# Third-group attention keys made by seven products in an earlier stage, with the scores woven into half projections

## The chip, the cores and the metric

The kernel runs on one core of a Trainium2 chip. The metric is the device time of one execution in microseconds; three runs of the kernel before gave 2182.49, 2182.76 and 2183.83 us, median 2182.76. A core has TensorE (PE, matrix products into PSUM; PEld are its weight loads), VectorE (DVE), ScalarE (ACT), GpSimd (POOL) and SyncE (SP, which here only issues DMAs). Each engine works through its own instructions in the order in which the program issued them, and waits on semaphores for the others.

## The reference

One decoder block on a sequence of 1024 tokens and width 1024, in float32: a token mixer and a squared-ReLU MLP, each behind an RMSNorm that is scaled and shifted by a conditioning vector. The mixer multiplies the normed input h by one wide matrix and cuts the result into retention queries, keys, values and gates (4 heads), attention queries, keys and values of three groups of 4 heads of 128 channels, and two gates. Cut to what matters here:

```
proj = h @ w_in
for gi, (win, dil) in enumerate(((128, 1), (512, 4), (2048, 16))):
    aq, ak, av = parts[4 + 3 * gi], parts[5 + 3 * gi], parts[6 + 3 * gi]
    # strided sub-sequences, banded blocks
    s = einsum(q, k) * dh ** -0.5 + bias
    mx = max(s); e = exp(s - mx); den = sum(e)
    o = einsum(e / den, v);  lse = mx + log(den)
wts = softmax over the three groups of lse
att = sum over groups of wts * o
att_out = att @ w_att_out
```

The kernel's "group 1" is the second one (dilation 4), "group 2" the third one (dilation 16), "group 0" the first.

## The kernel before, in words

A float32 product is made of three passes: both operands are split into a high part (a rounded copy, made by ScalarE) and a remainder (the difference, made by VectorE), and `mm3` (L203 to L211) issues low x high, high x low and high x high into one PSUM accumulation. A matmul takes 128 rows of weights by 512 tokens. A plain projection of one block of 128 channels, `proj_gen`, takes 8 slices of the width x 3 passes x 2 halves of the tokens = 48 matmuls.

The stages follow each other: values of attention; the **queries and keys stage** (`queries_keys`, L1212); retention values; 32 retention chunks; the **attention stage**; the gates and outputs; the MLP. They are one list of steps (`Steps`, L55). A step has loads of 512 KB tiles, each with a preparation (`split_w` for a weight, L194; `q_prep` for queries, L1475), and a body. All loads share three buffers (`wraw`) and go through SP's queue in order; a load is issued when the tile three places before it has been prepared (`issue`, L78). `following` (L114) issues the preparations of the next step, and of the step behind it the weights that come ahead of any other load, *before* the body of a step. So the splits of a step stand ahead of the body of the step before it in ScalarE's and VectorE's order.

**Queries and keys stage.** The stage computes two blocks of 128 channels at a time ("a pair") from a 2 x 2 blocking of weights and tokens by seven products of 12 matmuls, 84 in place of 96 (`Blocks`, L226; `ORDER`, L217 ff.). Per pair ScalarE and VectorE split 7 weight tiles of 512 columns (L254, L264), VectorE makes 4 sums of weights (L249) and combines the products (L286 to L293), and `a_out` (L1165) writes the four result blocks, for attention groups 1 and 2 in a strided order, and sends them to DRAM: retention queries and keys (`r`, behind which `rotate` applies the rotary embedding on VectorE, one instruction per product), attention queries (`a`, tiles `aqd`) and gates (`g`, sigmoid on ScalarE). `PAIRS` (L1136) gives the order of 18 pairs, "rargrargrargrargaa".

**Attention stage.** Heads are taken two by two ("attention pair" 0 and 1). For each of them there are six steps `att_step` (L1753), one for each group and head of `combos` (L1751): group 1, group 2, group 0, heads a = 0 and 1. A step projects the keys of its head with 48 matmuls, and weaves into them the scores of the head before (`weave`, from the third slice on: `lag=2`). `k_split` (L1484) then splits the keys out of PSUM. `scores_gen` (L1492) makes the scores bank by bank in four PSUM buffers and VectorE adds the bias (L1519, L1523); `scores_end` (L1526) reduces the maxima (L1529 to L1537), negates them (L1539) and lets ScalarE take eight exponentials (L1542). Queries come back from DRAM as loads. High and low parts of queries and keys live in a ring of 8 tiles (`ring`, L1405). After a group's second head `stats_out` (L1600) sends maxima and sums through DRAM on SP's queue. Behind the six steps come gate projections (`cover_step`, L1791: four in pair 0, three in pair 1). The first holds the last scores, then `weights` and `pscale` (L1645, L1647); the third holds the first group's weighted values (`weave_pv`, `pv_tr`, `pv_mm`: L1662 to L1688).

`with_sums` (L576) places one of 32 DMAs on POOL's queue after the second and the sixth slice of each projection; they add blocks of the retention output in DRAM (`result_sum`, L566).

Of the kernel before, what the change touches and what calls it, by code (L numbers as in the profile page):

```python
# [17 lines left out]
P = 128  # L18
# [122 lines left out]
def block_kernel(ctx, tc, io, stop=None, dbg=None):  # L141
# [24 lines left out]
    def ps_mm(name):  # L166
        return PS["p"].tile([P, 2, 512], F32, tag="mm", bufs=2, name=name)
# [314 lines left out]
    def at(gen, n, call):  # L482

        for i, _ in enumerate(gen):
            if i == n:
                call()
            yield
# [5 lines left out]
    def weave(main, n, fill, m, lag=0, rest=True):  # L493


        done = 0
        for i, _ in enumerate(main):
            while i >= lag and done * (n - lag) < (i + 1 - lag) * m:
                next(fill, None)
                done += 1  # L500
        if rest:
            drain(fill)
# [72 lines left out]

    def with_sums(gen):  # L576

        return at(at(gen, 1, result_sum), 5, result_sum)

    hd = {}  # L580
    NG = H * NC
# [187 lines left out]

    va_d = [dram.tile([S, 512], F32, name=f"vad{g}") for g in range(3)]  # L770
    aq_d = {(p, g, a): dram.tile([P, S], F32, name=f"aqd{p}{g}{a}") for p in range(2) for g in range(3) for a in range(2)}
    h12_d = [dram.tile([P, 2, 512], F32, name=f"h12d{m}") for m in range(4)]
    xn, wa = [], []

# [358 lines left out]
    r_pairs = [("r", t, h) for h in range(H) for t in "qk"]  # L1133
    a_pairs = [("a", g, p) for p in range(2) for g in range(3)]
    g_pairs = [("g", i) for i in range(len(GATES) // 2)]
    PAIRS = [{"r": r_pairs, "a": a_pairs, "g": g_pairs}[i].pop(0) for i in "rargrargrargrargaa"]  # L1136
    NA = len(PAIRS)
    OA = {}

    def a_load(q, part):  # L1140
        pair = PAIRS[q]
        src = io[{"g": "w_gate2", "a": "w_aq"}.get(pair[0]) or f"w_r{pair[1]}"]
        i = 2 * pair[1] + pair[2] if pair[0] == "a" else pair[-1]
        if q == 0 or q % 2 == 0 and part == 2:
            r = x4(f"wa{q}{part}")
        else:
            r = wraw.tile([P, 1024], F32, tag="raw", name=f"wa{q}{part}")
        nc.sync.dma_start(r, src[2 * i + part - 1])
        BA.raw[q, part] = r
# [15 lines left out]
    def a_out(q, n, x, y=None):  # L1165

        pair = PAIRS[q]
        if q not in OA:
            OA[q] = [x4(f"qa{q}{i}") for i in range(2)]
        i, t = int(n[0]) - 1, int(n[1]) - 1  # L1170
        o, view = OA[q][i][:, 512 * t:512 * t + 512], lambda z: z
        if pair[0] == "a" and pair[1] == 1:
            o = OA[q][i].rearrange("p (r n i) -> p r n i", r=4, n=2)[:, :, t, :]
            view = lambda z: z.rearrange("p (i r) -> p r i", r=4)
        elif pair[0] == "a" and pair[1] == 2:
            o = OA[q][i].rearrange("p (r i) -> p r i", r=8)[:, :, 64 * t:64 * t + 64]
            view = lambda z: z.rearrange("p (i r) -> p r i", r=8)
        f = AF.Sigmoid if pair[0] == "g" else AF.Copy
        if y is None:
            nc.scalar.activation(o, view(x), f)  # L1180
        else:
            (nc.vector.tensor_add if n == "12" else nc.vector.tensor_sub)(o, view(x), view(y))
            if pair[0] == "g":
                nc.scalar.activation(o, o, f)
        if n in ("12", "21"):
            if pair[0] == "g":
                dst = gate_d[GATES[2 * pair[1] + i]]
            elif pair[0] == "a":
                dst = aq_d[pair[2], pair[1], i]
            else:  # L1190
                return
            nc.sync.dma_start(dst, OA[q][i])
# [282 lines left out]
    def q_prep(pair, g, a):  # L1475
# [5 lines left out]
            A["q", g, a] = (hi, lo)  # L1481
        return prep

    def k_split(pair, g, a, ps):  # L1484

        hi, lo = ring(f"kh{pair}{g}{a}"), ring(f"kl{pair}{g}{a}")
        src, h_, l_ = by_blocks(ps, g), shaped(hi, g), shaped(lo, g)
        nc.scalar.copy(h_, src)
        nc.vector.tensor_sub(l_, src, fv(h_))
        A["k", g, a] = (hi, lo)  # L1490
# [70 lines left out]
    def v_fetch(pair, g):  # L1561

        for j in range(2):
            lo = A["l", g, j] = v_tile(pair, g, j, "vl")
            nc.sync.dma_start(fv(lo).rearrange("p (a b) -> p a b", a=4), v_rows(pair, g, j))
# [182 lines left out]
                done += 1  # L1748
        drain(main)

    combos = [(g, a) for g in (1, 2, 0) for a in range(2)]  # L1751

    def att_step(pair, i):  # L1753

        g, a = combos[i]

        def body(*args):
            ps = ps_mm(f"ak{pair}{i}")
            gen = with_sums(proj_gen(ps, args[-1]))
            if i == len(combos) - 2:  # L1760
                v_fetch(pair, 0)
            if i > 0:
                last = combos[i - 1]
                weave(gen, NK, scores_gen(pair, *last), len(SB[last[0]]), lag=2)
            elif pair == 0:
                args[0](1, True)
                for _ in range(4):
                    next(gen)
                on_T(H - 1, NC - 1)
                drain(gen)  # L1770
                u_final(H - 1)
                for h in range(H):
                    sums_left.extend(sums_of(h))
                open_att()
                args[0](3)
            else:

                gen = at(at(gen, 3, args[0]), NK - 1, lambda: k_split(pair, g, a, ps))
                weave_pv(gen, NK - 1, 0, 2)
            if i == 0:  # L1780
                A["st"] = A["p"].tile([P, 3, 8, 4], F32, tag="st", name=f"st{pair}")
                bias_load(pair)
            if i > 0 or pair == 0:
                k_split(pair, g, a, ps)
            if i > 0:
                scores_end(pair, *last)
                if last[1] == 1:
                    stats_out(pair, last[0])
        return body

    def cover_step(pair, n):  # L1791


        i = COVER[pair][n]

        def body(*args):
            ps = ps_mm(f"gate0{i}")
            gen = with_sums(proj_gen(ps, args[-1]))
            if n == 0:
                v_fetch(pair, 1)  # L1800
                weave(gen, 6, scores_gen(pair, *combos[-1]), len(SB[0]), lag=2, rest=False)
                drain(gen)
                v_split(pair, 0, False)
                scores_end(pair, *combos[-1])
                weights(pair)
                for a in range(2):
                    pscale(0, a)
            elif n == 1:
                drain(gen)
            elif n == 2:  # L1810
                v_fetch(pair, 2)

                gen = at(at(gen, 2, lambda: sigmoids(1)), 3, lambda: (args[0](3), v_split(pair, 1)))
                gen = at(gen, 6, sigmoids)
                weave_pv(gen, NK - 1, pair, 0)
                for a in range(2):
                    pscale(1, a)
            else:
                gen = at(at(gen, 3, lambda: [pscale(2, a) for a in range(2)]), 4, lambda: args[0](1))
                gen = at(at(at(gen, 6, lambda: v_split(pair, 2)), 6, args[0]), 6, sigmoids)  # L1820
                weave_pv(gen, NK - 1, pair, 1)
            if n > 1:
                t = A["r1"].tile([P, S], F32, tag="att", bufs=8, name=f"g0{i}s")
            else:
                t = ring(f"g0{i}s", F32)
            if n < 3:
                nc.vector.tensor_copy(t[:, :512], ps[:, 0])
                nc.scalar.copy(t[:, 512:], ps[:, 1])
                raw_gates.append((i, t))
            else:  # L1830
                nc.scalar.activation(t, flat(ps), AF.Sigmoid)
                nc.sync.dma_start(gate_d[i], t)
        return body
# [7 lines left out]
            nc.sync.dma_start(gate_d[i], t)  # L1841

    for pair in range(2):
        for i, (g, a) in enumerate(combos):
            steps.add(att_step(pair, i),
                      [wsplit(io["w_ak"][g * 4 + 2 * pair + a])] +
                      ([(aq_d[pair, *combos[i - 1]], q_prep(pair, *combos[i - 1]))] if i > 0 else []),
                      manual=("late" if pair else True) if i == 0 else False)
        for n in range(len(COVER[pair])):
            more = [(aq_d[pair, *combos[-1]], q_prep(pair, *combos[-1]))] if n == 0 else []  # L1850
            steps.add(cover_step(pair, n), more + [wsplit(io["w_gate"][len(COVER[0]) * pair + n])], manual={2: True, 3: "late"}.get(n, False))


# [897 lines left out]
def pack(x, c, w_ada, b_ada, norm1_g, w_in, rel_bias, ret_gn_g, ret_gn_b,  # L2751
# [16 lines left out]
        "w_rv": _vblocks(w[:, 2048:4096]),  # L2768
        "w_rg": _cols(w[:, 4096:6144]),
        "w_aq": _pairs(att[:, :, 0].reshape(1024, 1536)),  # L2770
        "w_ak": _cols(att[:, :, 1].reshape(1024, 1536)),
        "w_av": _vcols(att[:, 0, 2], 512),
        "w_av2": _vblocks(att[:, 1:, 2].reshape(1024, 1024)),
        "w_gate": _cols(gates(i for c in COVER for i in c)),
# [27 lines left out]
```

## Time and profile before

| | |
|---|---|
| median of three runs | 2182.76 us (2182.49 to 2183.83) |
| profiled execution | 2182.64 us, its span 2180.9 us |
| TensorE clock granted | 1.00 but for the start and the end |
| queries and keys stage | 180 to 523 us |
| attention stage, pair 0, six steps | 943.9 to 1024.6 us |
| attention stage, pair 1, first score step on | from 1111 us |
| HBM read, written | 319.93 MB, 156.13 MB |

A busy TensorE is a modelled figure: its matmuls overlap, so what counts is the distance from start to start. In an order of time each row has its start, duration, engine, line, operation and "output<-inputs", a count where rows are merged, and in brackets the idle time before it with what ended it. A row of DMA issues ends with the median microseconds from issue to landing.

### The profile page before, as it was taken

How to read it: one execution, taken by the hardware profiler on the slowest of the kernel's cores; microseconds unless marked ns; L12 is line 12 of the kernel's file. 1: busy time of each engine (PE TensorE's matmuls, PEld its weight loads, DVE VectorE, ACT ScalarE, POOL GpSimd, SP SyncE). 2: the span in 40 equal slices, each digit the busy share in tenths (PEclk: the TensorE clock that was granted, in tenths of full speed). 3: DMA queues.
4: the chain of work that ended last, by engine and by line, in shares of the span. 5: the costliest groups of instructions: out<-in, count | busy, mean ns of one | idle time of the engine just before them, and what ended most of it. 6: DMA issues, size and time to landing. Idle time of an engine off the chain costs nothing. (4 is left out here: it accounts for less than half of the span.)

```text
span 2180.9 us, 27323 instructions
## 1 busy us (share of the span) xinstructions
PE 2156.0 (99%) x10084; PEld 1791.6 (82%) x10084; DVE 1491.7 (68%) x2333; ACT 942.8 (43%) x1729; POOL 164.0 (8%) x195
## 2 busy tenths in 40 slices
PE   8999999999999999999999999999999999999998
PEld 6888888888878888888888888888778888888887
DVE  5985777774467877854655644776876665877855
ACT  5553323323434544544644625434454545533413
POOL 0001111100012212211100000001000000000003
PEclk9999999999999999999999999999999999999999
DMA  9859998844685555557763275654254435645322
GB/s 383 289 209 297 296 298 257 243 119 174 237 301 170 198 174 194 181 172 190 184 167 108 81 268 189 224 186 139 65 182 150 153 136 194 249 137 175 111 87 78
DMA packets 160881, 416.78 MB, mean 191 GB/s; under 512 B 27749, under 2 KB 55660, under 8 KB 157676
## 3 DMA queue, kind: packets, MB, share of 16 engines
q1 hardware_dynamic: 151416, 368.67, 47.9%
q0 software_dynamic: 9008, 46.14, 9.9%
q8 instruction: 79, 1.29, 0.2%
q14 instruction: 54, 0.44, 0.1%
q10 hardware_dynamic: 324, 0.23, 0.0%
HBM read 319.93 MB, written 156.13 MB: 218 GB/s over the span
## 5 line engine op out<-in xcount | busy, mean ns | idle before, releaser
L207 PE MATMUL qap<-hh,qaw 128*128 128x512 f32 x216 | 84.0, 389 | 0.0
L209 PE MATMUL qap<-hl,qaw 128*128 128x512 f32 x216 | 84.0, 389 | 0.0
L211 PE MATMUL qap<-hh,qaw 128*128 128x512 f32 x216 | 84.0, 389 | 0.0
L617 POOL TENSOR_TENSOR j<-qk,j 128x512 fp32r<-128x512 f32 x32 | 43.2, 1351 | 412.4 <-ACT j L616 393.8
L2122 POOL TENSOR_TENSOR accnf<-accnf,sqnf 128x256 f32<-128x256 f32 (+1 forms) x18 | 16.6, 922 | 609.9 <-ACT sqnf L2118 609.9
L2226 ACT ACTIVATE a<-a 128x512 f32<-128x512 f32 x48 | 30.3, 631 | 73.7 <-DVE a L2225 73.7
L1542 ACT ACTIVATE P<-P,ng 128x128 f32<-128x128 f32 (+1 forms) x96 | 42.0, 439 | 36.6 <-DVE ng L1539 36.6
L2434 ACT CAST w2h<-w2s 128x512 fp32r<-128x512 f32 x36 | 22.4, 622 | 78.7 <-DVE w2s L2472 78.7
L264 DVE TENSOR_TENSOR fw<-w1r,fw 128x512 fp32r<-128x512 f32 x48 | 32.9, 688 | 33.6 <-ACT fw L254 33.6
L1957 DVE TENSOR_TENSOR rwl<-rwl,rwh 128x1024 fp32r<-128x1024 f32 x25 | 30.2, 1220 | 29.1 <-ACT rwh L1987 29.1
L207 PE MATMUL fp<-h2h,fw 128*128 128x512 f32 x128 | 50.0, 391 | 0.0
L211 PE MATMUL fp<-h2h,fw 128*128 128x512 f32 x128 | 49.8, 389 | 0.0
L209 PE MATMUL fp<-h2l,fw 128*128 128x512 f32 x128 | 49.8, 389 | 0.0
L207 PE MATMUL roa<-rh,rwl 128*128 128x512 f32 x128 | 49.8, 389 | 0.0
L209 PE MATMUL roa<-rl,rwh 128*128 128x512 f32 x128 | 49.8, 389 | 0.0
L211 PE MATMUL roa<-rh,rwh 128*128 128x512 f32 x128 | 49.8, 389 | 0.0
L652 ACT COPY sm<-sT 128x128 f32<-128x128 f32 x32 | 8.5, 266 | 93.7 <-PE sT L640 93.7
L207 PEld LDWEIGHTS qap<-hh,qaw 128*128 128x128 f32 x216 | 40.5, 188 | 8.5
L209 PEld LDWEIGHTS qap<-hl,qaw 128*128 128x128 f32 x216 | 40.5, 188 | 8.4
L211 PEld LDWEIGHTS qap<-hh,qaw 128*128 128x128 f32 x216 | 40.5, 188 | 8.4
L2122 POOL TENSOR_TENSOR accn<-accn,sqn 128x512 f32<-128x512 f32 x12 | 15.5, 1293 | 386.1 <-ACT sqn L2118 386.1
L1947 ACT ACTIVATE rh<-rl 128x512 fp32r<-128x512 f32 x56 | 31.7, 623 | 23.4 <-PE roc L209 8.4
(3097 smaller groups left out, 7251.4 us busy)
## 6 DMA issues: line engine op xcount, KB each, us to landing
v<-vd SPq DMA_DIRECT2D x32, 512.0 KB, 4.5
raw<-in_w_ada_dram SPq DMA_DIRECT2D x32, 512.0 KB, 5.3
w1r<-in_w_ff_dram SPq DMA_DIRECT2D x32, 512.0 KB, 4.6
yt<-y POOLq DMA_DIRECT2D x24, 512.0 KB, 7.6
xsd<-as SPq DMA_DIRECT2D x24, 512.0 KB, 2.8
w2r<-in_w_ff2s_dram SPq DMA_DIRECT2D x24, 512.0 KB, 6.9
em<-in_w_ada_dram SPq DMA_DIRECT2D x16, 512.0 KB, 10.2
wrvs<-in_w_rv_dram POOLq DMA_DIRECT2D x16, 512.0 KB, 10.0
```

The source lines that it names most:

```text
L207: nc.tensor.matmul(o, wl, xh, start=first, stop=False, skip_group_check=skip)
L209: nc.tensor.matmul(o, wh, xl, start=False, stop=False, skip_group_check=skip)
L211: nc.tensor.matmul(o, wh, xh, start=False, stop=last, skip_group_check=skip)
L264: nc.vector.tensor_sub(t[:, 512:], src, fv(t[:, :512]))
L617: nc.gpsimd.tensor_sub(t[:, 1], src, fv(t[:, 0]))
L652: nc.scalar.copy(sm, ps[:, :C])
L1542: nc.scalar.activation(v, v, AF.Exp, bias=ng[:, blk:blk + 1], accum_out=st[:, g, blk, 2 + a:3 + a])
L1947: nc.scalar.activation(hi, fv(lo), AF.Copy, scale=sign)
L1957: nc.vector.tensor_sub(lo, fv(lo), fv(hi))
L2122: (nc.vector if f == 7 else nc.gpsimd).tensor_add(G["acc", key], G["acc", key], sq)
L2226: nc.scalar.activation(o, o, AF.Relu)
L2434: nc.scalar.copy(hi, src)
```

## The change

The keys of group 2 are taken out of the attention stage. Two `k` pairs in the queries and keys stage make them by seven products (weights in a new layout, `w_ak2`), in the strided order of that group, and store them in DRAM (`akd`). In the attention stage they come back as loads with a preparation of their own, `k_prep`.

So an attention pair has four key projections instead of six. Group 1's two stay whole steps. Group 0's two are cut into halves of four slices (`att_first`, `att_second`), and each half takes one head's scores, woven in from the second slice on (`lag=1`): group 1 head 1, group 2 head 0, group 2 head 1, group 0 head 0. The last scores stay in the first gate projection. The order of `PAIRS` changes too: 20 pairs, two gates moved to the end. `with_sums` places three sums per projection. The host only packs the weights.

```diff
-        return at(at(gen, 1, result_sum), 5, result_sum)
+        return at(at(at(gen, 1, result_sum), 3, result_sum), 5, result_sum)
...
-    PAIRS = [{"r": r_pairs, "a": a_pairs, "g": g_pairs}[i].pop(0) for i in "rargrargrargrargaa"]
+    k_pairs = [("k", 2, p) for p in range(2)]
+    PAIRS = [{"r": r_pairs, "a": a_pairs, "g": g_pairs, "k": k_pairs}[i].pop(0) for i in "rargrarkrargrarkgaga"]
...
-        elif pair[0] == "a" and pair[1] == 2:
+        elif pair[0] in "ak" and pair[1] == 2:
...
+            elif pair[0] == "k":
+                dst = ak_d[pair[2], i]
...
+    def k_prep(pair, a):
+
+        def prep(raw):
+            hi, lo = ring(f"kh{pair}2{a}"), ring(f"kl{pair}2{a}")
+            nc.scalar.copy(hi, raw)
+            nc.vector.tensor_sub(lo, raw, fv(hi))
+            A["k", 2, a] = (hi, lo)
+        return prep
...
+    HALF = NK // 2
+
+    def att_first(pair, a):
+
+        def body(*args):
+            A["kp"] = ps_mm(f"ak{pair}0{a}")
+            A["kg"] = with_sums(proj_gen(A["kp"], args[-1]))
+            done = (1, 1) if a == 0 else (2, 1)
+            if a == 1:
+                v_fetch(pair, 0)
+            weave(itertools.islice(A["kg"], HALF), HALF, scores_gen(pair, *done), len(SB[done[0]]), lag=1)
+            scores_done(pair, *done)
+        return body
+
+    def att_second(pair, a):
+
+        def body(*args):
+            done = (2, 0) if a == 0 else (0, 0)
+            weave(A["kg"], HALF, scores_gen(pair, *done), len(SB[done[0]]), lag=1)
+            k_split(pair, 0, a, A["kp"])
+            scores_done(pair, *done)
         return body
...
-        for i, (g, a) in enumerate(combos):
-            steps.add(att_step(pair, i),
-                      [wsplit(io["w_ak"][g * 4 + 2 * pair + a])] +
-                      ([(aq_d[pair, *combos[i - 1]], q_prep(pair, *combos[i - 1]))] if i > 0 else []),
-                      manual=("late" if pair else True) if i == 0 else False)
...
+        steps.add(att_step(pair, 0), [w_load(1, 0)], manual="late" if pair else True)
+        steps.add(att_step(pair, 1), [w_load(1, 1), q_load(1, 0)])
+        steps.add(att_first(pair, 0), [w_load(0, 0), q_load(1, 1)])
+        steps.add(att_second(pair, 0), [q_load(2, 0), k_load(0)])
+        steps.add(att_first(pair, 1), [w_load(0, 1), q_load(2, 1), k_load(1)])
+        steps.add(att_second(pair, 1), [q_load(0, 0)])
```

`scores_done` is `scores_end` followed by `stats_out` after a group's second head.

More of the change, by code (lines that the diff above doesn't have):

```diff
@@ L771, in block_kernel @@
     aq_d = {(p, g, a): dram.tile([P, S], F32, name=f"aqd{p}{g}{a}") for p in range(2) for g in range(3) for a in range(2)}
+    ak_d = {(p, a): dram.tile([P, S], F32, name=f"akd{p}{a}") for p in range(2) for a in range(2)}
     h12_d = [dram.tile([P, 2, 512], F32, name=f"h12d{m}") for m in range(4)]
@@ L1141, in a_load @@
         pair = PAIRS[q]
-        src = io[{"g": "w_gate2", "a": "w_aq"}.get(pair[0]) or f"w_r{pair[1]}"]
+        src = io[{"g": "w_gate2", "a": "w_aq", "k": "w_ak2"}.get(pair[0]) or f"w_r{pair[1]}"]
         i = 2 * pair[1] + pair[2] if pair[0] == "a" else pair[-1]
@@ L1171, in a_out @@
         o, view = OA[q][i][:, 512 * t:512 * t + 512], lambda z: z
-        if pair[0] == "a" and pair[1] == 1:
+        if pair[0] in "ak" and pair[1] == 1:
             o = OA[q][i].rearrange("p (r n i) -> p r n i", r=4, n=2)[:, :, t, :]
             view = lambda z: z.rearrange("p (i r) -> p r i", r=4)
-        elif pair[0] == "a" and pair[1] == 2:
+        elif pair[0] in "ak" and pair[1] == 2:
             o = OA[q][i].rearrange("p (r i) -> p r i", r=8)[:, :, 64 * t:64 * t + 64]
@@ L1749, in weave_pv, with scores_done, att_step @@
         drain(main)
-    combos = [(g, a) for g in (1, 2, 0) for a in range(2)]
-    def att_step(pair, i):
-        g, a = combos[i]
+    def scores_done(pair, g, a):
+        scores_end(pair, g, a)
+        if g > 0 and a == 1:
+            stats_out(pair, g)
+    def att_step(pair, a):
         def body(*args):
-            ps = ps_mm(f"ak{pair}{i}")
+            ps = ps_mm(f"ak{pair}1{a}")
             gen = with_sums(proj_gen(ps, args[-1]))
[L1760 to L1764, printed above, removed]
+            if a == 1:
+                weave(gen, NK, scores_gen(pair, 1, 0), len(SB[1]), lag=2)
             elif pair == 0:
@@ L1776, in body @@
             else:
-                gen = at(at(gen, 3, args[0]), NK - 1, lambda: k_split(pair, g, a, ps))
+                gen = at(at(gen, 3, args[0]), NK - 1, lambda: k_split(pair, 1, 0, ps))
                 weave_pv(gen, NK - 1, 0, 2)
-            if i == 0:
+            if a == 0:
                 A["st"] = A["p"].tile([P, 3, 8, 4], F32, tag="st", name=f"st{pair}")
                 bias_load(pair)
[L1783 to L1788, printed above, removed]
+            if a == 1 or pair == 0:
+                k_split(pair, 1, a, ps)
+            if a == 1:
+                scores_done(pair, 1, 0)
+        return body
[5 more added lines that the diff above has]
+            done = (1, 1) if a == 0 else (2, 1)
+            if a == 1:
+                v_fetch(pair, 0)
+            weave(itertools.islice(A["kg"], HALF), HALF, scores_gen(pair, *done), len(SB[done[0]]), lag=1)
+            scores_done(pair, *done)
+        return body
+    def att_second(pair, a):
[4 more added lines that the diff above has]
+            scores_done(pair, *done)
         return body
@@ L1800, in body @@
                 v_fetch(pair, 1)
-                weave(gen, 6, scores_gen(pair, *combos[-1]), len(SB[0]), lag=2, rest=False)
+                weave(gen, 6, scores_gen(pair, 0, 1), len(SB[0]), lag=2, rest=False)
                 drain(gen)
                 v_split(pair, 0, False)
-                scores_end(pair, *combos[-1])
+                scores_end(pair, 0, 1)
                 weights(pair)
@@ L1843, in block_kernel, with q_load, k_load, w_load @@
     for pair in range(2):
-        for i, (g, a) in enumerate(combos):
-            steps.add(att_step(pair, i),
-                      [wsplit(io["w_ak"][g * 4 + 2 * pair + a])] +
-                      ([(aq_d[pair, *combos[i - 1]], q_prep(pair, *combos[i - 1]))] if i > 0 else []),
-                      manual=("late" if pair else True) if i == 0 else False)
+        def q_load(g, a):
+            return aq_d[pair, g, a], q_prep(pair, g, a)
+        def k_load(a):
+            return ak_d[pair, a], k_prep(pair, a)
+        def w_load(g, a):
+            return wsplit(io["w_ak"][g * 4 + 2 * pair + a])
+        steps.add(att_step(pair, 0), [w_load(1, 0)], manual="late" if pair else True)
[4 more added lines that the diff above has]
+        steps.add(att_second(pair, 1), [q_load(0, 0)])
         for n in range(len(COVER[pair])):
-            more = [(aq_d[pair, *combos[-1]], q_prep(pair, *combos[-1]))] if n == 0 else []
+            more = [q_load(0, 1)] if n == 0 else []
             steps.add(cover_step(pair, n), more + [wsplit(io["w_gate"][len(COVER[0]) * pair + n])], manual={2: True, 3: "late"}.get(n, False))
@@ L2770, in pack @@
         "w_aq": _pairs(att[:, :, 0].reshape(1024, 1536)),
-        "w_ak": _cols(att[:, :, 1].reshape(1024, 1536)),
+        "w_ak": _cols(att[:, :2, 1].reshape(1024, 1024)),
+        "w_ak2": _pairs(att[:, 2, 1]),
         "w_av": _vcols(att[:, 0, 2], 512),
```

## The prediction

> **What bounds the kernel now.** I read the page's busy times first, then the windows of the two stages that the change touches, then ScalarE's, VectorE's and TensorE's order of time in the first attention pair.
>
> ```profile
> span 2180.9 us, 27323 instructions
> PE 2156.0 (99%) x10084; PEld 1791.6 (82%) x10084; DVE 1491.7 (68%) x2333; ACT 942.8 (43%) x1729; POOL 164.0 (8%) x195
> ```
> ```profile
> 180.00:523.00 343.00, 343.00 (x1515) 284.02 (x1514) 245.29 (x382) 100.01 (x174) 36.31 (x50) 1.00 0.79 238
> 969.60:1049.50 79.90, 79.90 (x410) 68.00 (x409) 45.70 (x77) 41.21 (x121) 9.41 (x14) 1.00 0.74 199
> 1122.40:1202.30 79.90, 79.90 (x411) 67.98 (x410) 43.99 (x74) 41.27 (x121) 0.82 (x1) 1.00 0.34 96
> 2175.00:2181.00 6.00, 0.00 (x0) 0.00 (x0) 1.97 (x4) 0.00 (x0) 0.00 (x0) 0.50 0.58 193
> ```
>
> The columns of a window are its length and the busy time (count) of PE, weight loads, DVE, ACT, POOL, then granted clock, DMA share and GB/s. TensorE is the bound everywhere: it is busy in all of the queries and keys stage (180 to 523) and in all of both attention stretches (the second and third row: from the third key product of a pair to its third gate product, 79.9 us each). 343.00 us for 1515 matmuls of 512 columns is **0.2264 us a matmul**. A change is worth what it takes off TensorE, as long as nobody makes TensorE wait.
>
> **The change, part by part.**
>
> *Matmuls.* Two pairs with seven products enter the queries and keys stage: 2 x 84 x 0.2264 = **+38.0 us**. Four full projections of 48 leave the attention stage: 192 x 0.2264 = **-43.5 us**. The difference is 24 matmuls, 5.4 us.
>
> *The queries and keys stage.* Does it take two more pairs at TensorE's pace?
>
> ```profile
> L1182 DVE TENSOR_TENSOR qa<-qat,qap x36: 677/686/1133, 192.6 to 523.0; 128x512 f32<-128x512 f32 x36
> ```
>
> A pair gives VectorE 4 sums, 7 remainders, 2 differences and 3 results, 16 x 0.69 = 11.0 us, and for the third group's strided order 3 x 0.45 more (1133 against 686 ns), 12.4 us of the pair's 84 x 0.2264 = 19.0. The rotation of the retention pair before it, 12 instructions spread over 14 products, puts up to 7 x 0.69 = 4.8 us beside it: 17.2 of 19.0, which the present pair of third-group queries behind a retention pair already bears without a TensorE gap. The gates that now end the list add sigmoids to ScalarE, which is busy for 100 of 343 us. SP issues two loads and two stores more per pair, as for any other pair. So +38.0 stands; if a product did come late, it would be by one VectorE instruction, 0.7 us, a few times.
>
> *The attention stage.* Here the 96 matmuls a pair that leave were also the cover for the scores. The next rows are ScalarE, VectorE and TensorE in the first pair.
>
> ```profile
> 978.01 1.04 ACT L1479 ACTIVATE qh<-raw 128x1024 fp32r<-128x1024 f32 x1
> 988.08 0.40 ACT L1542 ACTIVATE P<-P,ng 128x128 f32<-128x128 f32 x1 [3.22 <-DVE ng L1539]
> 991.61 1.04 ACT L1479 ACTIVATE qh<-raw 128x1024 fp32r<-128x1024 f32 x1
> 992.56 1.03 ACT L197 CAST raw_8378h<-raw 128x1024 fp32r<-128x1024 f32 x1
> 1001.19 0.40 ACT L1542 ACTIVATE P<-P,ng 128x128 f32<-128x128 f32 x1 [2.63 <-DVE ng L1539]
> 1004.29 1.05 ACT L1479 ACTIVATE qh<-raw 128x1024 fp32r<-128x1024 f32 x1
> 1029.68 0.41 ACT L1542 ACTIVATE P<-P,ng 128x128 f32<-128x128 f32 x1 [3.62 <-DVE ng L1539]
> 1033.53 1.04 ACT L197 CAST raw_8707h<-raw 128x1024 fp32r<-128x1024 f32 x1
> 1040.64 0.40 ACT L1542 ACTIVATE P<-P,ng 128x128 f32<-128x128 f32 x1 [4.17 <-DVE ng L1539]
> ```
> ```profile
> 981.36 1.88 DVE L1519 TENSOR_TENSOR P<-sc,bias 128x512 f32<-128x512 f32 x3
> 986.04 0.68 DVE L1534 TENSOR_REDUCE st<-P 128x4 f32<-128x512 f32 x1
> 992.69 1.23 DVE L1480 SCALAR_TENSOR_TENSOR ql<-raw,qh 128x1024 fp32r<-128x1024 f32 x1 [4.64 <-ACT qh L1479]
> 993.83 1.22 DVE L198 TENSOR_TENSOR raw_8378l<-raw,raw_8378h 128x1024 fp32r<-128x1024 f32 x1
> 994.97 1.28 DVE L1519 TENSOR_TENSOR P<-sc,bias 128x512 f32<-128x512 f32 x2
> 998.60 1.23 DVE L1489 TENSOR_TENSOR kl<-ak,kh 128x1024 fp32r<-128x1024 f32 x1 [2.35 <-ACT kh L1488]
> 999.74 1.21 DVE L1537 TENSOR_REDUCE st<-P 128x8 f32<-128x1024 f32 x1
> 1022.46 1.88 DVE L1519 TENSOR_TENSOR P<-sc,bias 128x512 f32<-128x512 f32 x3
> 1024.26 0.61 DVE L1523 TENSOR_TENSOR P<-sc,bias 128x256 f32<-128x256 f32 x2
> 1027.23 0.28 DVE L1529 TENSOR_REDUCE st<-P 128x1 f32<-128x128 f32 x1
> ```
> ```profile
> 997.30 0.62 PE L207 MATMUL ak<-hh,raw_8268l 128*128 128x512 f32 x2
> 1010.98 0.62 PE L207 MATMUL ak<-hh,raw_8378l 128*128 128x512 f32 x2
> 1054.51 0.39 PE L1687 MATMUL pv<-ptl000(0, 0, 0)_9051,vh 128*128 128x256 f32 x1 [0.34 <-DVE ptl000(0, 0, 0)_9051 L1667]
> ```
>
> The reader is to see a **loop through two engines**. The splits of the next step are issued ahead of a step's own scores, so the order is: ScalarE copies the high parts, VectorE takes the remainders, then VectorE adds the bias to the scores that TensorE made meanwhile, reduces them, ScalarE takes eight exponentials, and only behind these come the next copies (qh starts at 991.61 and 1004.29, where the exponentials end). The brackets are where an engine of the loop waits for the other one or for TensorE. Now each turn has a step of 1010.98 - 997.30 = 13.7 us of TensorE. In the changed kernel four of the steps have 24 matmuls and one head's scores: 13.7 - 24 x 0.2264 = 8.25 us. The copies that a turn holds are not fewer: the third group's keys come from DRAM and are split in place of its weights.
>
> From the rows, from start to start: first copy to first remainder 1.08; a remainder 1.14; a bias addition 0.60 (2.41 for the first group's five); the split of a product's keys on VectorE 1.14 (998.60 to 999.74); reduction to first exponential 2.04 for the second group (986.04 to 988.08), 1.45 for the third (999.74 to 1001.19), 2.45 for the first (1027.23 to 1029.68); exponentials 3.53, 3.10 and 3.85 (988.08 to 991.61, 1001.19 to 1004.29, 1029.68 to 1033.53). The turns of the changed kernel, from the end of the first head's exponentials:
>
> - A, three splits (third-group query and key, a weight), scores of the second group: 1.08 + 3 x 1.14 + 3 x 0.60 + 2.04 + 3.53 = 11.9
> - B, two splits, third group, keys of a product: 1.08 + 2.28 + 1.20 + 1.14 + 1.45 + 3.10 = 10.2
> - C, one split, third group: 1.08 + 1.14 + 1.20 + 1.45 + 3.10 = 8.0
> - D, three splits (a query, two gate weights), first group, keys of a product: 1.08 + 3.42 + 2.41 + 1.14 + 2.45 + 3.85 = 14.4
> - E, one split, first group, up to its first exponential: 1.08 + 1.14 + 2.41 + 2.45 = 7.1
>
> Together **51.5 us** with no idle time, of which TensorE wanted four times 8.25 for A to D. Before, the same way is 1040.64 - 978.01 = 62.6 us, idle time included. From the exponential at 1040.64 to the weighted values at 1054.51 the rest of the chain runs without a pause, and TensorE already waits 0.34 us at its end. So a pair becomes 62.6 - 51.5 = **11.1 us** shorter, although 96 x 0.2264 = 21.7 us of matmuls leave it: TensorE waits some 10.6 us more per pair. Laid against TensorE's order: about 0.6 us at the third group's first scores, 3.9 at its second, 1.1 at the first group's first, 3.7 at the first gate product (its weight is split last but one in D), 0.5 at the first group's second scores, and the rest at the first weighted values.
>
> *Loads.*
>
> ```profile
> raw<-aqd SPq DMA_DIRECT2D x5, 512.0 KB, 6.3
> raw<-in_w_gate_dram SPq DMA_DIRECT2D x4, 512.0 KB, 7.6
> std<-st SPq DMA_DIRECT2D x2, 16.0 KB, 4.4
> ```
>
> The raw tiles have three buffers, and a load starts when the tile three before it has been split. The third-group loads of turn B start in A, some 9 us before their copies, against 6.3. The second gate weight waits for the query remainder of C (24.4 us into the chain) and lands at 24.4 + 7.6 = 32.0, just when its copy is due (A + B + C + two copies = 32.0). SP's queue also stands behind a statistics store that waits for A's exponentials, and behind its read-back; the query load queued there lands at about 11.9 + 4.4 + 6.3 = 22.6 or a little later, and is due at D's start, 30.1. The lateness of that gate weight goes straight into the chain: between 0 and about 3 us a pair; I take 0.75, 1.5 us for both.
>
> *The rest at nothing:* a third result sum per projection (POOL runs these as its DMAs land, not as TensorE goes), eight more SP issues, 4 MB more of traffic.
>
> **Sum**, against the profiled execution (2180.9 us span, 2182.64 us in all; the median of the runs is 2182.76): +38.0 - 2 x 11.1 + 1.5 = +17.3, which gives 2200 us.
>
> **The rivals.**
>
> *The two engines keep up.* If the turns fit into 8.25 us, all 24 matmuls are won: 2182.6 - 5.4 = 2177. For it: ScalarE is busy for half and VectorE for 57% of the stretches. Against: that is a share, and the rows show the work in series; it decides where a mean turn of A to D (44.5 / 4 = 11.1 us) passes 8.25. Chance 0.08.
>
> *Half of it is hidden:* splits that reach the front of the queues earlier than I think, say 5 us less wait a pair: 2190. Chance 0.09.
>
> *Loads come late,* with ten of them in some 10 us less and DMA at 0.74 already: 3 us in two places a pair in place of the 1.5 above, 2182.6 + 15.8 + 12 = 2210. Chance 0.12.
>
> *The clock falls.* The last window above shows a granted clock of 0.50 once TensorE is idle, and 1.00 wherever it is busy. A matmul at half the clock costs 0.23 us more, so some 3.4 us of slow work behind each of the four longest waits would cost 1.7 each, 6.8 at most: 2207. Most of it would fall into the waits that follow, where the two other engines are late anyway. The Trainium skill, "TensorE: Matmul & The Clock Gate", Part 1, says that an idle window of about 3.4 us halves the clock until a busy one has passed; waits of 3.7 and 3.9 us are at that edge. Chance 0.04.
>
> *The queries stage doesn't take the pairs:* with 17.2 of 19.0 us on VectorE against, +2 to +4 on top, 2203. Chance 0.03, inside my range. The forecast itself gets 0.64.
>
> **Numbers.** 2200 us; its own terms reach from 2194 (hand-offs shorter by 0.3 us a turn, no late load) to 2206 (3 us a pair). With late loads and the slower clock above and part of the hidden case below, **2193 to 2211**. What a measurement can tell from no change is 0.2%, 4.4 us: faster 0.08, within it 0.05, slower 0.87.
>
> **What would show it.** Right: a queries and keys stage 38 us longer with TensorE still busy throughout; in each attention pair TensorE waits for ScalarE's copies and VectorE's remainders of third-group queries and keys and of the first gate weight, about 10 us; ScalarE's exponentials and copies back to back; some 52 us from the second group's first exponentials' end to the first exponential of the first group's second head. Wrong: TensorE fully busy there, or long waits that end with a DMA.

## The result and the profile after

The changed kernel takes 2201.24 us (median of six runs, 2200.03 to 2202.39), the kernel before 2182.95 us in the six runs beside it: 18.3 us slower, ratio 1.0084 with a 95% interval of 1.0071 to 1.0097. The forecast was 2200. The profiled execution took 2201.57 us, with a span of 2199.8.

First the page of the kernel after, its head and its busy times:

```profile
span 2199.8 us, 27353 instructions
PE 2163.6 (98%) x10060; PEld 1796.2 (82%) x10060; DVE 1509.7 (69%) x2361; ACT 949.0 (43%) x1743; POOL 163.9 (7%) x195
```

TensorE has 24 matmuls fewer (10060 against 10084) and yet shows 7.6 us more busy time: some of its work must have run slower. Keep that for the windows below.

The stages come out of the views by tile, which give the first and the last start of a group. Here the products of the queries and keys stage (`qap`), the first retention gate (`rg`), the first key projection (`ak`) and the first output projection (`ao`), in the kernel before:

```profile
L211 PE MATMUL qap<-hh,qaw x216: 389/389/389, 180.6 to 519.9; 128*128 128x512 f32 x108
L207 PE MATMUL rg<-hh,raw_4761l x16: 387/391/481, 631.6 to 651.5; 128*128 128x512 f32 x16
L207 PE MATMUL ak<-hh,raw_7930l x16: 389/389/481, 944.1 to 954.4; 128*128 128x512 f32 x16
L207 PE MATMUL ao<-ah,raw_10088l x16: 389/389/500, 1250.7 to 1261.5; 128*128 128x512 f32 x16
```

The same rows of the kernel after:

```profile
L211 PE MATMUL qap<-hh,qaw x240: 389/389/389, 181.8 to 559.2; 128*128 128x512 f32 x120
L207 PE MATMUL rg<-hh,raw_5025l x16: 389/394/500, 671.9 to 692.1; 128*128 128x512 f32 x16
L207 PE MATMUL ak<-hh,raw_8194l x16: 389/389/481, 984.7 to 994.9; 128*128 128x512 f32 x16
L207 PE MATMUL ao<-ah,raw_10169l x16: 389/389/497, 1269.5 to 1280.3; 128*128 128x512 f32 x16
```

Distances between these starts:

| stretch | before | after | difference |
|---|---|---|---|
| start to the first of these products of the queries stage | 180.6 | 181.8 | +1.2 |
| queries and keys stage, first to last | 339.3 | 377.4 | **+38.1** |
| last of it to first retention gate (the values) | 111.7 | 112.7 | +1.0 |
| retention | 312.5 | 312.8 | +0.3 |
| attention stage, `ak` to `ao` | 306.6 | 284.8 | **-21.8** |
| rest of the span | 930.2 | 930.3 | +0.1 |

Together +18.9, which is the difference of the spans. The attention stage gives back 21.8 us although 192 x 0.2264 = 43.5 us of matmuls left it.

The windows of the kernel after (columns as in the prediction; the queries and keys stage, pair 0, in it the stretch of lower clock, pair 1 and two such stretches in it):

```profile
180.00:560.60 380.60, 380.60 (x1681) 315.15 (x1680) 267.76 (x414) 110.11 (x192) 36.23 (x50) 1.00 0.74 225
1010.20:1080.00 69.80, 64.61 (x319) 54.47 (x317) 44.36 (x76) 40.46 (x121) 8.58 (x13) 0.93 0.78 211
1034.80:1045.00 10.20, 10.20 (x37) 8.94 (x37) 5.93 (x9) 4.13 (x17) 1.34 (x2) 0.50 0.76 160
1150.00:1233.00 83.00, 77.41 (x405) 65.61 (x403) 49.54 (x83) 48.84 (x132) 2.16 (x3) 0.94 0.49 136
1174.80:1181.60 6.80, 6.00 (x21) 5.26 (x22) 4.82 (x7) 2.55 (x11) 0.00 (x0) 0.50 0.41 101
1195.20:1198.60 3.40, 3.40 (x10) 2.62 (x9) 3.40 (x7) 0.00 (x0) 0.00 (x0) 0.50 1.01 373
```

The first row shows TensorE busy for the whole queries and keys stage. In the attention pairs it loses time in two forms. Idle: 69.80 - 64.61 = 5.2 us in pair 0, 83.00 - 77.41 = 5.6 in pair 1. And half speed: at a granted clock of 0.50, half of the busy time is loss, 10.20 / 2 = 5.1 us in pair 0 and (6.00 + 3.40) / 2 = 4.7 in pair 1. Both together are **10.3 us in each pair**. Whoever adds up the listed waits alone finds only half of it.

ScalarE's order of time in pair 0 gives the loop. For each turn these are its first copy, behind the exponentials of the turn before, and its first exponential:

```profile
1019.06 1.04 ACT L1483 ACTIVATE qh<-raw 128x1024 fp32r<-128x1024 f32 x1
1027.51 0.40 ACT L1555 ACTIVATE P<-P,ng 128x128 f32<-128x128 f32 x1 [5.52 <-DVE ng L1552]
1031.04 1.04 ACT L1483 ACTIVATE qh<-raw 128x1024 fp32r<-128x1024 f32 x1
1038.17 0.40 ACT L1555 ACTIVATE P<-P,ng 128x128 f32<-128x128 f32 x1 [4.24 <-DVE ng L1552]
1041.26 1.04 ACT L1483 ACTIVATE qh<-raw 128x1024 fp32r<-128x1024 f32 x1
1046.25 0.40 ACT L1555 ACTIVATE P<-P,ng 128x128 f32<-128x128 f32 x1 [3.95 <-DVE ng L1552]
1049.35 1.04 ACT L1483 ACTIVATE qh<-raw 128x1024 fp32r<-128x1024 f32 x1
1059.73 0.40 ACT L1555 ACTIVATE P<-P,ng 128x128 f32<-128x128 f32 x1 [6.05 <-DMA raw<-in_w_gate_dram]
1063.59 1.03 ACT L197 CAST raw_8890h<-raw 128x1024 fp32r<-128x1024 f32 x1
1070.68 0.40 ACT L1555 ACTIVATE P<-P,ng 128x128 f32<-128x128 f32 x1 [4.17 <-DVE ng L1552]
```

The turns start at 1019.06, 1031.04, 1041.26, 1049.35 and 1063.59: 12.0, 10.2, 8.1, 14.2 and, to 1070.68, 7.1 us. Each time the next copy follows the last exponential at once, and each time the first exponential ends a wait for VectorE. One bracket misleads: at 1059.73 it names a load of a gate weight. VectorE's order of time shows what came just before:

```profile
1059.53 0.17 DVE L1552 TENSOR_SCALAR ng<-st 128x8 f32<-128x8 f32 x1
```

The negated maxima end at 1059.70, so it was VectorE here too.

The three longest of TensorE's own waits in the attention stage of the kernel after, summed (us in total, times, longest), and its gaps at the second head of the third group:

```profile
PE sc L207 <- DVE ql L1484: 5.2, 2, 2.6
PE sc L209 <- DVE kl L1493: 1.9, 4, 0.7
PE gate L207 <- DVE raw_10002l L198: 1.8, 1, 1.8
```
```profile
1033.48 0.30 PE L207 MATMUL sc<-kh,ql 128*128 128x128 f32 x1 [2.58 <-DVE ql L1484]
1034.53 0.33 PE L209 MATMUL sc<-kl,qh 128*128 128x128 f32 x1 [0.75 <-DVE kl L1493]
```

The long waits end with VectorE's remainders of third-group queries and keys, as the prediction wanted to see, and the stretch of half clock begins right behind them, at 1034.80. Another 1.25 us of the idle time in pair 0 is no such wait: at 1079.90 the third gate product stands behind ScalarE's copy of the first gate out of PSUM.

### The profile page after: what moved, and what is told of

Same layout as the page of the kernel before. It is cut to its first block, busy times and chain, and to the rows that moved or that the text cites. A ratio compares the mean times of both kernels' runs of the same rounds, so it can differ in the third digit from the quotient of the medians.

```text
span 2199.8 us, 27353 instructions
## 1 busy us (share of the span) xinstructions
PE 2163.6 (98%) x10060; PEld 1796.2 (82%) x10060; DVE 1509.7 (69%) x2361; ACT 949.0 (43%) x1743; POOL 163.9 (7%) x195
## 5 line engine op out<-in xcount | busy, mean ns | idle before, releaser
L207 PE MATMUL qap<-hh,qaw 128*128 128x512 f32 x240 | 93.4, 389 | 0.0
L209 PE MATMUL qap<-hl,qaw 128*128 128x512 f32 x240 | 93.4, 389 | 0.0
L211 PE MATMUL qap<-hh,qaw 128*128 128x512 f32 x240 | 93.4, 389 | 0.0
L211 PEld LDWEIGHTS qap<-hh,qaw 128*128 128x128 f32 x240 | 45.0, 188 | 9.4
L209 PEld LDWEIGHTS qap<-hl,qaw 128*128 128x128 f32 x240 | 45.0, 188 | 9.4
L207 PEld LDWEIGHTS qap<-hh,qaw 128*128 128x128 f32 x240 | 45.0, 188 | 9.3
L292 DVE TENSOR_TENSOR qat<-qat,qap 128x512 f32<-128x512 f32 x20 | 13.7, 687 | 48.8 <-PE qap L211 48.8
L264 DVE TENSOR_TENSOR qaw<-wa,qaw 128x512 fp32r<-128x512 f32 x60 | 39.9, 685 | 7.4 <-ACT qaw L254 7.4
## 6 DMA issues: line engine op xcount, KB each, us to landing
em<-in_w_ada_dram SPq DMA_DIRECT2D x16, 512.0 KB, 10.2
wrvs<-in_w_rv_dram POOLq DMA_DIRECT2D x16, 512.0 KB, 10.2
```

The lines of the kernel that those rows point to most:

```text
L207: nc.tensor.matmul(o, wl, xh, start=first, stop=False, skip_group_check=skip)
L209: nc.tensor.matmul(o, wh, xl, start=False, stop=False, skip_group_check=skip)
L211: nc.tensor.matmul(o, wh, xh, start=False, stop=last, skip_group_check=skip)
L264: nc.vector.tensor_sub(t[:, 512:], src, fv(t[:, :512]))
L292: nc.vector.tensor_sub(u, u, b)
```

## The experiments

The theory: each attention pair is bound by the serial loop ScalarE, VectorE, ScalarE, and TensorE has room in it. Its rivals: TensorE or the clock is the bound; late loads are; or the price lies in the two new pairs. e1 and e6 start from the kernel before, the others from the one after.

| run | median (range), us | ratio to before (95%) |
|---|---|---|
| e1_pairs_only | 2222.61 (2221.98 to 2223.36) | 1.0181 (1.0167 to 1.0195) |
| e2_remainder_twice | 2205.43 (2204.05 to 2207.13) | 1.0102 (1.0088 to 1.0116) |
| e3_extra_products | 2200.27 (2199.83 to 2202.32) | 1.0080 (1.0066 to 1.0094) |
| e4_exps_later | 2193.26 (2190.88 to 2193.91) | 1.0044 (1.0030 to 1.0058) |
| e5_gates_later | 2182.45 (2180.42 to 2184.98) | 1.0000 (0.9991 to 1.0009) |
| e6_before_remainder_twice | 2183.26 (2182.03 to 2184.13) | 1.0002 (0.9993 to 1.0011) |
| e7_keys_first | 2185.75 (2181.74 to 2188.32) | 1.0012 (1.0003 to 1.0021) |
| e8_clock_kept | 2190.23 (2186.29 to 2192.80) | 1.0029 (1.0017 to 1.0041) |

**The two pairs alone** (in the kernel before; the keys are stored and not used):

```diff
-    PAIRS = [{"r": r_pairs, "a": a_pairs, "g": g_pairs}[i].pop(0) for i in "rargrargrargrargaa"]
+    k_pairs = [("k", 2, p) for p in range(2)]
+    PAIRS = [{"r": r_pairs, "a": a_pairs, "g": g_pairs, "k": k_pairs}[i].pop(0) for i in "rargrarkrargrarkgaga"]
```

> The kernel before with the two key pairs in the queries and keys stage (order of pairs as changed, keys stored in DRAM and not used); the attention stage still makes all keys itself, so it does more than needed. If that stage takes the pairs at TensorE's pace: before + 168 x 0.2264 = +38.0 us, 2221, the stage 38.1 us longer without a TensorE wait. If the pairs or their traffic cost more (the changed kernel came to the attention stage 40.5 us later, 1.3 of it between the values and the attention stage and 1.2 ahead of the queries): +40 to +42, with the same waits there.

Measured +39.5 us. Its rows by tile:

```profile
L211 PE MATMUL qap<-hh,qaw x240: 389/389/389, 180.7 to 558.1; 128*128 128x512 f32 x120
L207 PE MATMUL rg<-hh,raw_5025l x16: 387/394/499, 670.8 to 691.0; 128*128 128x512 f32 x16
L207 PE MATMUL ak<-hh,raw_8194l x16: 389/389/481, 983.6 to 993.8; 128*128 128x512 f32 x16
L207 PE MATMUL ao<-ah,raw_10352l x16: 389/389/501, 1290.1 to 1300.9; 128*128 128x512 f32 x16
```

The stage is 558.1 - 180.7 = 377.4 us as in the kernel after, the values take 112.7 as there, and the attention stage 306.5 as before. So the two halves of the change add up, and the +1.0 in the values belongs to the pairs (or to their new order), not to the attention stage. The +39.5 lies between the two expectations: the stage takes the pairs at TensorE's pace, and 1.0 us in the values and 0.3 in retention come on top.

**VectorE's remainder of the third group's keys issued twice** (four instructions more in all), in the kernel after and, as a control (e6), for the third group's keys in the kernel before:

```diff
             nc.vector.tensor_sub(lo, raw, fv(hi))
+            nc.vector.tensor_sub(lo, raw, fv(hi))
```
```diff
+        if g == 2:
+            nc.vector.tensor_sub(l_, src, fv(h_))
```

> The changed kernel with VectorE's remainder of the third group's keys made twice (four more instructions of 1.2 us; same output). If the loop of ScalarE and VectorE bounds the attention stage, each lies on it: 4 x 1.14 = +4.6 us on the changed kernel, 2205.8. If TensorE's clock or its matmuls bound it, or late loads: no change, 2201.

> The kernel before with VectorE's remainder of the third group's keys made twice, the same four instructions as in e2. There the loop has slack under whole projections: no change on the kernel before, 2183 (at most +1). If any VectorE work in the stage counted, as with a bound on VectorE alone: +4.6.

Measured +4.2 us on the kernel after, where 4 x 1.14 = 4.6 were expected (its runs lie wholly above those of the kernel after), and +0.4 on the kernel before, which is inside its interval around no change. The attention stage of e2:

```profile
L207 PE MATMUL ak<-hh,raw_8194l x16: 389/389/481, 983.1 to 993.3; 128*128 128x512 f32 x16
L207 PE MATMUL ao<-ah,raw_10173l x16: 389/389/499, 1272.5 to 1283.2; 128*128 128x512 f32 x16
```

That is 289.4 us, 4.6 more than the 284.8 of the kernel after; in e6 it is 1250.3 - 943.8 = 306.5, as before. An instruction on VectorE that cost nothing before goes into the time in full after the change. That is a loop without slack.

**More work for TensorE** (48 matmuls into PSUM that is overwritten later, 12 at two places of each pair: 10.9 us):

```diff
+            if a == 1:
+                extra(A["kp"], args[-1])
...
+            if a == 1:
+                A["gps"] = ps_mm(f"gate0{COVER[pair][0]}")
+                extra(A["gps"], A["kw"])
```

> The changed kernel with 48 more matmuls of 512 columns, 12 ahead of the second half-projected head and 12 behind it in each attention pair, into PSUM that is overwritten afterwards (same output). 48 x 0.2264 = 10.9 us of TensorE work. If TensorE waits there for the loop anyway: 0 to +1.5 us on the changed kernel, 2201 to 2203, and the clock stays nearer to 1.00. If TensorE's own time counts there: +10.9, 2212.

Measured 2200.27, 1.0 us below the kernel after and inside its range. Its windows of the two pairs:

```profile
1010.00:1080.00 70.00, 66.10 (x345) 55.17 (x344) 44.01 (x77) 40.97 (x121) 8.07 (x12) 1.00 0.80 212
1150.00:1233.00 83.00, 78.98 (x423) 66.21 (x422) 50.59 (x84) 49.83 (x133) 2.15 (x3) 1.00 0.49 134
```

TensorE has 5.4 us more work per pair, the clock stays at 1.00 throughout, and the time is the same. Alone this does not rule TensorE out: 5.4 us of work came in where about 5 us of half-speed loss went, so that TensorE's own time hardly changed. ScalarE's rows decide it, the first copy and the last exponential of the same chain in pair 0:

```profile
1017.85 1.04 ACT L1483 ACTIVATE qh<-raw 128x1024 fp32r<-128x1024 f32 x1
1069.57 0.41 ACT L1555 ACTIVATE P<-P,ng 128x128 f32<-128x128 f32 x1 [4.22 <-DVE mx L1630]
```

These are 51.7 us, against 51.6 in the kernel after, and each turn agrees within 0.1. So the loop keeps its pace with the clock at 1.00 and at 0.50, and TensorE still stands idle for 70.00 - 66.10 = 3.9 us in pair 0 and 4.0 in pair 1. TensorE was not the bound, and the half clock of the kernel after cost nothing that these runs show: it lay inside the wait for the loop.

**The exponentials issued later:** the reduction and the exponentials of a step go behind the splits that follow them, to the front of the next body, so that ScalarE's copies no longer wait for them.

```diff
+    def scores_later(*which):
+        A["later"] = which
+
+    def scores_now():
+        scores_done(*A.pop("later"))
...
-            scores_done(pair, *done)
+            scores_later(pair, *done)
```

> The changed kernel with one change of order: a head's reductions and exponentials are issued after the splits of the next step, so that these don't stand behind them in ScalarE's and VectorE's order. Work, loads and matmuls are the same. If the order in the loop is the cause: 8 to 9.5 us less wait in each attention pair, 2201 - 18 = 2183 (2181 to 2187), with some 3 us of wait left at the first group's second head. If loads or the clock cause the waits: 2198 to 2202.

Measured 2193.26: 8 us fewer where 18 were expected. So the order costs time, but something else came next. Its attention stage (278.3 us), its longest waits in sum, ScalarE and TensorE at the longest, and the window of half clock there:

```profile
L207 PE MATMUL ak<-hh,raw_8194l x16: 389/389/481, 983.5 to 993.7; 128*128 128x512 f32 x16
L207 PE MATMUL ao<-ah,raw_10155l x16: 389/389/497, 1261.8 to 1272.7; 128*128 128x512 f32 x16
```
```profile
PE sc L207 <- ACT kh L1501: 9.0, 2, 6.1
```
```profile
1045.41 1.05 ACT L197 CAST raw_8799h<-raw 128x1024 fp32r<-128x1024 f32 x1 [4.13 <-DMA raw<-in_w_gate_dram]
1052.19 0.99 ACT L1501 CAST kh<-ak 128x1024 fp32r<-128x1024 f32 x1
```
```profile
1053.23 0.58 PE L207 MATMUL sc<-kh,ql 128*128 128x256 f32 x1 [6.08 <-ACT kh L1501]
```
```profile
1049.70:1059.90 10.20, 5.99 (x19) 5.12 (x20) 7.03 (x11) 6.39 (x25) 1.32 (x2) 0.50 0.81 194
```

ScalarE stands for 4.13 us in front of the second gate weight, which has not landed; the exponentials and the copy of the last keys stand behind it, and TensorE behind these. This is the late load of the prediction, which appears once the loop is shorter. And where TensorE works on, it does so at half the clock until 1059.9: 5.99 us of work, of which half is loss.

**The gate weights split later too:** the second inside the first gate step, the fourth behind the first weighted values. (A step marked manual issues preparations only where its body asks for them.)

```diff
+            if a == 1:
+                args[0](3)
...
-        steps.add(att_second(pair, 1), [q_load(0, 0)])
+        steps.add(att_second(pair, 1), [q_load(0, 0)], manual=True)
...
-manual={2: True, 3: "late"}.get(n, False))
+manual={1: True, 2: True, 3: "late"}.get(n, False))
```

> The order of e4, and the second gate weight of each attention pair split a step later (in the first gate projection, with the third), the last one behind the first weighted values. In e4 ScalarE waited 4.1 us for that weight's landing and the keys' split behind it held TensorE for 6.1 us. If that load was what was left: some 2 us of wait per pair, an attention stage of 267 us in place of 278, 2182 (2180 to 2185), clock near 1.00. If other loads or the weighted values take its place: 2187 to 2193.

Measured 2182.45, as expected. Its first key projection starts at 984.7, as in the kernel after; its first output projection and its longest waits:

```profile
L207 PE MATMUL ao<-ah,raw_10231l x16: 389/389/504, 1250.6 to 1261.4; 128*128 128x512 f32 x16
```
```profile
PE sc L209 <- DVE kl L1502: 2.5, 4, 0.9
PE sc L207 <- ACT kh L1501: 1.1, 1, 1.1
```

The stage takes 265.9 us, against 306.6 - 43.5 = 263.1 if no wait came in for the matmuls that left. So 40.7 of the 43.5 us are won, 18.9 more than in the kernel after: by order alone, with the same work on every engine. It ties the kernel before, since the attention stage begins 984.7 - 944.1 = 40.6 us later than there. Splitting the gate weights later without the first change of order was not tried; an estimate from the chain's rows is one remainder, 1.14 us, less in each pair.

**The last keys ahead of the third group's exponentials** (on top of that, for the 2.5 + 1.1 us):

```diff
-            scores_now()
+            else:
+                scores_now()
...
+            if a == 1:
+                scores_now()
```

> As e5, with the keys of the first group's second head split ahead of the third group's last exponentials instead of behind them. If the order in ScalarE's queue decides: the last 2 us of wait per pair before those scores go and up to 0.6 comes back at the weighted values, 2180 (2178 to 2183). If the exponentials moved back are then late for the statistics' way through DRAM: 2183 or more, with waits on the statistics.

A miss: 2185.75, scattered over 6.6 us. In the trace the waits for the keys went, and others came two steps later, at the gate products that wait for the copies of gates out of PSUM, not on the statistics:

```profile
PE gate L207 <- ACT g00s L1875: 2.7, 1, 2.7
PE gate L207 <- ACT g04s L1875: 1.9, 1, 1.9
```

The traced run took 2182.12 us, the second fastest of eleven and no longer than e5's median, so these waits don't show where the median lost 3 us. The granted clock over the whole run goes with the time: 0.999 in the three fastest runs, 0.996 in the four slowest. Which wait brings it down was not traced, and the cause stays open.

**TensorE kept busy in the long wait** (on the kernel with the later exponentials; 36 matmuls, 8.2 us, into PSUM that the gate projection overwrites):

```diff
+            if a == 1:
+                A["gps"] = ps_mm(f"gate0{COVER[pair][0]}")
+                extra(A["gps"], A["kw"], 4 - 2 * pair)
```

> The kernel with the exponentials issued later, and TensorE kept busy where it would wait: 24 extra matmuls in the first attention pair and 12 in the second, ahead of the first gate projection and into its PSUM, which that projection then overwrites (36 x 0.2264 = 8.2 us of work for TensorE; the output is not changed). In that kernel (2193.3 us) the granted clock was 0.50 for 10.2 us in the first pair and 6.8 us in the second, with TensorE the bound behind the wait. Theory 1, the half clock cost time there: the half-speed work behind the wait, some 6.7 us in the first pair (1053.2 to 1059.9) took twice its time, so some 3 us a pair come back: 2186 to 2191, with a granted clock of 1.00 in both stretches. Theory 2, the half clock lay in idle time and cost nothing: 2193 to 2196, clock 1.00 too. Theory 3, TensorE's work itself counts there, not the wait for the copy: +8.2, 2201.

Measured 2190.23: 3.0 us *fewer* with 8.2 us more work, at the upper end of theory 1, but the six runs scatter and the intervals of the two ratios overlap. Its trace says more than its time (the attention stage, then windows of the two pairs behind the extra work):

```profile
L207 PE MATMUL ak<-hh,raw_8194l x16: 389/389/481, 984.4 to 994.7; 128*128 128x512 f32 x16
L207 PE MATMUL ao<-ah,raw_10179l x16: 389/389/500, 1259.1 to 1269.9; 128*128 128x512 f32 x16
```
```profile
1049.70:1064.00 14.30, 11.24 (x50) 9.09 (x50) 10.45 (x16) 8.83 (x34) 1.32 (x2) 0.88 0.74 226
1180.00:1200.00 20.00, 20.00 (x106) 17.13 (x105) 15.54 (x22) 13.16 (x39) 0.00 (x0) 1.00 0.62 199
```

274.7 us against 278.3. In pair 1 the clock stays at 1.00; in pair 0 a mean of 0.88 over 14.30 us is 14.30 x 0.12 x 2 = 3.4 us at half clock, where the kernel without the extra work had 10.2. That a clock that stays up is worth 3 to 4 us here is what these two traces suggest; the scattered runs do not show it, and the expected 1.00 in both pairs was not reached. The run does rule out theory 3: 8.2 us of work did not add 8.2 us.

## Why the prediction was right

- **Queries and keys stage:** forecast +38.0, measured +38.1 in the kernel after and alone (e1), with TensorE busy for 380.60 of 380.60 us. The rival in which the stage doesn't take the pairs is out.
- **The loop:** forecast for the turns 11.9, 10.2, 8.0, 14.4 and 7.1, in all 51.5 us; measured 12.0, 10.2, 8.1, 14.2 and 7.1, in all 51.6 (in pair 1, from 1160.57 to 1212.22, 51.65). A sum of rows of before, in the new order, gave it. That it is serial was not only argued: VectorE's instruction counts in full there and not before (e2, e6), the loop keeps its pace when TensorE's work and clock change (e3), and another order alone takes 18.8 us off (e4, e5).
- **TensorE's loss:** forecast 10.6 us a pair, measured 10.3, but half as waits and half as matmuls at half clock. The places of the waits were forecast roughly: 3.9 at the third group's second head was 2.58 + 0.75, 3.7 at the first gate product was nothing listed in pair 0 and 1.8 in pair 1.
- **The late load, +1.5: mis-sized.** It cost nothing here, in either pair. The copy of that gate weight came 1051.23 - 1019.06 = 32.2 us into the chain, just behind its estimated landing at 32.0, with no idle time before it; the row in question:

```profile
1051.23 1.05 ACT L197 CAST raw_8810h<-raw 128x1024 fp32r<-128x1024 f32 x1
```

  With this term left out the attention stage was forecast at -22.2, and came at -21.8. The rival in which loads come late was thus not the case, but its mechanism is real: 4.13 us as soon as the loop is shorter (e4).
- **Not foreseen:** +1.0 in the values, +0.3 in retention, and +1.2 ahead of the queries stage, 2.5 together. The last isn't the change's: the same start lies at 180.7 in e1 and in e3, as in the kernel before within 0.1, and between 180.5 and 181.8 over all ten traces. For the first a row of the groups by form shows the wait:

```profile
L207 PE MATMUL rg<-hh,raw_5025l 128*128 128x512 f32 x16 | 5.3, 415 | 0.8 <-DVE vr L1322 0.8
```

  VectorE is late with the last retention values. The wait is there in e1 too, and not in the kernel before; why the pairs bring it was not tried, and stays open.
- **The clock** fell, as that rival had it, behind shorter waits than it named (2.58 and 1.83 us) and for longer than it said (10.2 us in pair 0 in place of 3.4 behind a wait), but it cost nothing, since the half-speed work lay where TensorE would have waited (e3: no half clock, the same turns, the same time). **Engines that keep up** and **half of it hidden** are out: no turn was shorter than forecast by more than 0.2 us.

So the forecast missed by 1.2 us: a load term 1.5 too high against some 2.5 of small stretches that no row of before showed. The loop, which carries the forecast, was worked out; that the miss is so small is in part luck, since these two cancel in part.

## What to carry to other kernels

Before taking matmuls out of a stage, ask what their time covers: write down one turn of the loop through the other engines from rows of the trace, in issue order, and compare its length with what is left of TensorE's. If the turn is longer, look at the order of issue ahead of the amount of work: here copies that stood behind exponentials cost 18.8 us, and moving them gave it all back in two steps, because the first uncovered a load. And count matmuls at half clock with the waits, or half of a stall is missed.

## What the runs showed of the hardware

The granted clock fell to 0.50 in stretches of 3.4, 6.8 and 10.2 us, multiples of 3.4. The Trainium skill, "TensorE: Matmul & The Clock Gate", Part 1, gives a free-running window of about 3.4 us after which an idle one halves the clock; the lengths agree. Two things go beyond its table. The window need not be empty: the clock fell at 1034.80 behind waits of 2.58 and 0.75 us with a matmul of 0.30 us between them, 3.3 us of idle time in all, and at 1195.20 behind a single wait of 1.83 us, with TensorE busy for the other 1.57 of the 3.40 us. And the table has the clock back after one or more busy windows, but one was not always enough: from 1034.80 to 1045.00 TensorE shows busy for all of the 10.20 us, and the clock stayed at 0.50, while at 1198.60 it was back after 3.40 us. The second stretch holds only matmuls of 512 columns; whether the short score products of 128 columns, which make up about half of the first, count for less was not tried.
